# Recording the program and issuing it in a list scheduler's order, in place of a weave with fitted step times

## The chip, the cores and the metric

One core of one Trainium2 chip runs one program. The metric is the device time of that program in microseconds; the kernel before was run three times, with a median of 1408.34 us (1407.92 to 1408.75). The engines named below are PE (TensorE: matmuls, with PEld for its weight loads), DVE (VectorE), ACT (ScalarE), POOL (GpSimd) and SP (which only issues DMAs). Each takes its own instructions strictly in the order in which the program gives them to it, and waits on semaphores for the others.

## The reference

One layer of a diffusion backbone on 1024 latent tokens of 1024 channels, with 256 context tokens:

```python
h_x = layer_norm(x) * (1 + scale_x) + shift_x              # adaLN from c; the same for ctx
p_x = split(h_x @ w_in)                                    # f_val, f_gate, qkv, dn_gate, beta, decay, r_f, r_d
y_f = fourier_branch(p_x[0], p_x[1])                       # 4 groups: Re(2-D DFT), linear map, SiLU gate, projection
y_d = deltanet_branch(qkv, dn_gate, beta, decay)           # 8 heads of 128, two directions
out = (sigmoid(r_f) * y_f + sigmoid(r_d) * y_d) @ w_out
x   = layer_norm(2**0.25 * x + gate_x * out) * ln_g + ln_b
```

The DeltaNet branch takes a short convolution and SiLU of q, k and v, and then, in chunks, solves a unit triangular system per chunk, direction and head, and scans the chunks with a 128x128 state:

```python
a_mat = strict_tril(kb @ k.T * decay) + I                  # per chunk
u, w  = triangular_solve(a_mat, [v * beta, kb * exp(gc)])
for chunk:                                                 # scan
    v_new = u - w @ S
    o     = (q * exp(gc)) @ S + qk @ v_new
    S     = S * exp(g_last) + k_dec.T @ v_new
```

The latent scans start from the final states of the context scans. All is in float32.

## The kernel before, in words

The program has three parts, one after the other, each with its own pool of on-chip buffers in the place of the last one's. **Head and Fourier branch**: `head` loads the tokens and adaLN's weights, normalises, transposes and modulates them into an operand of eight row blocks in two parts (`hh`, `hl`); then the context's k and v, the Fourier branch's blocks and its projections run. **DeltaNet heads** (pool `dn`): eight heads, one after the other. **Tail**: the DeltaNet output projection, the merge, the output projection and the last layer norm.

A product with weights is done in "blocks" of 128 output channels by 1024 tokens (`latent`, L192): 8 contraction steps by 2 halves by 3 passes (`mm3y`, L124: lines L127, L130 and L133), 48 matmuls of 512 columns into a `main` tile, of which PSUM holds two. Their weights come by `weight` (L178): a 512 KB load, a cast by ACT in two halves (L188), and a subtraction by POOL (L189); two sets of buffers.

A head's own work is a chain (`deltanet` L671, `inverse` L724, `scan` L818):

- `zp` (L688 on PE, L692 on DVE) from k, q and the decay factors E, which `decays` (L703) loads from DRAM (L708), masks on POOL (L710) and exponentiates on ACT (L714). E has four buffers for a head's five pairs of chunks.
- `inverse`: a stream transpose into X (L736), 30 steps of DVE (L748, L751), a transpose back (L755), two rounds of small matmuls 32 to 64 (L774, L784, with transposes L789 and L790 behind them), and two rounds 64 to 128 (L802, L810) with copies by ACT between them.
- `scan`: ten steps. Each is PE (L840), DVE (R, L842), PE (L854), ACT (L856), PE (L869), DVE (S, L873), in two directions side by side, with L850, L861, L863 and L881 beside it.

`zp`, `kdec`, `acc`, `ktok` and the state tiles have one buffer, so the next head's `zp` starts when this scan is done. While the chain of head h runs, the program also does the projections of head h+1 (k, q, v, and the output gate of head h) with their convolutions, norms and transposes (`qkv_jobs`, L596), and one, two or five of the sixteen merge blocks (`TAKE`): mostly six blocks a head. The end of head h-1 (`finish`, L893) is done within head h's X steps.

What sets the order around the change: Python writes instructions in program order, and that is the order on each engine. The chain is a generator that yields where PE may take other work; the blocks are a second generator that yields after every three matmuls. `weave` (L248) runs the chain to its next yield, looks up that yield's entry in a table of fitted times (`STEPS`, 89 entries; `STEPS_LAST` for head 7; `TABLES` for the gate tables; `FIN` for the end), times a fitted factor per head (`RATES`), and issues block matmuls worth that many microseconds. Whatever a block brings with it on DVE, ACT, POOL and SP is written at the place where its last matmul falls.

```python
        for _ in lead:
            owed += next(times) * rate
            while owed > 0:
                q = next(fill, None)
                ...
                owed -= q
```

Of the kernel before, what the change touches and what calls it, by code (L numbers as in the profile page):

```python
# [27 lines left out]
TABLES = (9.2, 8.15, 1.41, 5.3)  # L28
STEPS_LAST = (0.354, 0.604, 2.165, 0.754, 0.454, 1.602, 0.427, 0.511, 1.07, 1.452, 0.19, 0.0, 0.694, 1.883, 0.935, 0.771, 1.001, 1.231, 0.803, 1.117, 1.529, 1.062, 0.606, 1.002, 0.821, 0.0, 0.776, 0.623, 0.595, 0.854, 0.526, 0.486, 0.182, 0.492, 2.076, 0.247, 1.65, 0.0, 0.0, 0.0, 0.0, 1.894, 0.04, 0.0, 0.0, 0.0, 2.162, 0.0, 0.38, 0.0, 1.134, 0.15, 0.821, 0.0, 0.0, 0.377, 0.12, 0.0, 1.081, 0.378, 0.0, 0.54, 0.77, 0.0, 0.54, 0.378, 0.242, 0.6, 0, 0.269, 0.45, 0.57, 0.269, 0.0, 0.378, 0.569, 1.0, 0.12, 0.269, 0.4, 0.378, 0.242, 0.648, 0.574, 0.722, 0.0, 1.0, 0.269, 2.7)
STEPS = (0.204, 0.604, 0.604, 0.604, 0.604, 1.187, 0.427, 0.511, 1.07, 0.662, 0.19, 1.19, 0.844, 2.033, 0.785, 0.921, 0.851, 1.231, 0.803, 1.267, 1.979, 0.0, 1.056, 1.614, 0.821, 0.8, 0.776, 0.623, 0.595, 0.854, 0.826, 0.486, 0.332, 0.042, 1.276, 0.397, 1.65, 0.0, 0.0, 0.0, 0, 1.426, 0.04, 0.0, 0.468, 0.0, 2.162, 0.8, 0.0, 0.0, 1.134, 0.0, 0.021, 0.0, 0.0, 0.135, 0.27, 0.0, 0.931, 0.378, 0.392, 0.54, 0.378, 0.242, 0.84, 0.078, 0.242, 0.6, 0.0, 0, 0.45, 0.57, 0.538, 0.0, 0.378, 0.569, 0.55, 0.77, 0.269, 0.6, 0.378, 0.242, 0.39, 1.378, 1.202, 0.12, 0.0, 1.1, 3.119)  # L30
FIN = 0.292
RATES = (0.966, 1.34, 1.34, 1.34, 1.34, 1.23, 1.666, 1.33)
# [30 lines left out]

class Net:
    def __init__(self, tc, es, a, out, dbg=None):
        self.tc, self.es, self.a, self.out = tc, es, a, out
        self.nc = tc.nc
        self.dbg = dbg or {}

    def pool(self, name, bufs=1, es=None, **kw):  # L70
        return (es or self.es).enter_context(self.tc.tile_pool(name=name, bufs=bufs, **kw))

    def dump(self, name, ap, idx=None):
        if name in self.dbg:
            dst = self.dbg[name]
            if idx is not None:
                dst = dst[idx]
            if ap.dtype == F32R:
                ap = ap.bitcast(F32)
            self.nc.sync.dma_start(out=dst, in_=ap)  # L80

# [1 line left out]
    def rsqrt(self, pool, x, shape, tag):  # L83
        """1 / sqrt(x) of a small float32 tile: Newton steps from an integer seed."""
# [32 lines left out]
    def mm3(self, ps, lh, ll, rh, rl, first, last):  # L117
        """ps += (lh + ll)^T (rh + rl) in three float32r passes."""
# [5 lines left out]
    def mm3y(self, ps, lh, ll, rh, rl, first, last):  # L124
        """The same, giving TensorE away in between."""
# [11 lines left out]
    def constants(self):  # L137
# [21 lines left out]
        # adds up four blocks of 32 rows  # L159
# [32 lines left out]
    def latent(self, src, rhs, k, done):  # L192
        """A block of weights times the latent tokens' operand: quanta of PE work, then done(PSUM)."""
# [24 lines left out]
    def plain(self, f):  # L218
        """Work that needs no weights, as a job."""
        def job(w):  # L220
            f()
            yield 0.0
        return None, 0, job

    def after(self, f):
        """The same for work in several parts."""
        return None, 0, lambda w: f()

    def stream(self, jobs, first=None):
        """Run jobs in order, the weights of the next one under way; first: the first one's, if they are."""  # L230
# [17 lines left out]
    def weave(self, lead, fill, rate, times):  # L248
        """fill takes TensorE between the lead's steps: after each, rate times its entry of times."""
        owed = 0.0  # L250
        times = iter(times)
        for _ in lead:
            owed += next(times) * rate
            while owed > 0:
                q = next(fill, None)
                if q is None:
                    owed = float("-inf")
                    break
                owed -= q

# [1 line left out]
    def pe_add(self, x, rows, ec, eng=None):  # L262
        """x += the tokens' position code: the grid's rows in one half of the channels, its columns in the other."""
# [1120 lines left out]
```

## Time and profile before

| what | value |
|---|---|
| time, median of 3 runs | 1408.34 us |
| span of the profiled execution | 1409.0 us, no time of its own beside it |
| PE busy | 1296.9 us (92%) |
| PE weight loads busy | 1050.7 us (75%) |
| DVE busy | 967.8 us (69%) |
| ACT, POOL busy | 555.9, 451.1 us |
| granted PE clock, mean of the span | 0.959 |
| DMA | 129.91 MB, 92 GB/s |

How to read it: a matmul's record runs from its start to a modelled end, and consecutive matmuls overlap, so that PE's busy share counts time in which a matmul is still draining and no next one has started. What PE needs is read from the distance between starts in a dense stretch. The chain of waits follows back from the last instruction to what released each one.

### The profile page before, as it was taken

Reading aid. Unit: us, or ns where it says so; the run is one execution under the profiler, and the core shown is the slowest. Engines: PE = TensorE matmul, PEld = TensorE weight load, DVE = VectorE, ACT = ScalarE, POOL = GpSimd, SP = SyncE. Lnnn points to the kernel's source line nnn. Section 1 sums busy time; section 2 is a strip of 40 time slices with the busy share of each in tenths; the row PEclk is TensorE's granted clock in tenths of the full one; section 3 lists DMA queues with packets and bytes.
Section 4 is the critical chain, followed back from the end, with each engine's and each line's share of the span. In section 5 each row is a group of like instructions: output and inputs, shape, how many; then the busy total and the mean of one; then the engine's idle time right before and its main releaser. Section 6 shows DMA issues by size and latency. Waiting matters only on the chain.

```text
span 1409.0 us, 22686 instructions
## 1 busy us (share of the span) xinstructions
PE 1296.9 (92%) x8274; PEld 1050.7 (75%) x8274; DVE 967.8 (69%) x2664; ACT 555.9 (39%) x1499; POOL 451.1 (32%) x358
## 2 busy tenths in 40 slices
PE   7899999999789989889899998988998999999997
PEld 1487787887678768768777876876876877888786
DVE  6776554308876965984894795697697494744997
ACT  2643333335444444443544444345354343521200
POOL 3532332135523222430440332223243122234610
PEclk9999999999899999989998999999998999999999
DMA  8434332342211211311311211121120032375431
GB/s 316 152 97 119 115 111 91 125 169 78 65 39 44 69 46 48 88 61 38 83 58 56 53 62 66 50 79 54 35 79 31 31 113 75 120 264 162 160 124 60
DMA packets 51892, 129.91 MB, mean 92 GB/s; under 512 B 6242, under 2 KB 18915, under 8 KB 51780
## 3 DMA queue, kind: packets, MB, share of 16 engines
q1 hardware_dynamic: 44496, 114.02, 26.1%
q10 hardware_dynamic: 7284, 14.45, 3.0%
q8 instruction: 65, 1.06, 0.3%
q14 instruction: 47, 0.39, 0.1%
HBM read 105.29 MB, written 23.15 MB: 91 GB/s over the span
## 4 chain that ended last, share of the span: by engine, by line
PE 50%; DVE 33%; DMA 6%; ACT 5%; POOL 3%; issue 3%; ACTq 0%; SPq 0%; DVEq 0%; POOLq 0%
PE main L127 8%; PE main L133 8%; PE main L130 8%; DVE X L751 7%; DVE B L748 6%; DMA E<-gr 3%; PE s L854 3%; PE s L869 3%; PE s L840 2%; PE s L881 2%; PE s L850 2%; DVE cv L553 2%; POOL E L710 2%; DVE cv L552 2%; PE main L120 2%
## 5 line engine op out<-in xcount | busy, mean ns | idle before, releaser
L127 PE MATMUL main<-h,whi 128*128 128x512 f32 x1008 | 424.8, 421 | 6.2 <-DVE cv L553 6.2
L133 PE MATMUL main<-h,wlo 128*128 128x512 f32 x1008 | 410.8, 408 | 0.1
L130 PE MATMUL main<-l,whi 128*128 128x512 f32 x1008 | 410.2, 407 | 0.0
L127 PEld LDWEIGHTS main<-h,whi 128*128 128x128 f32 x1008 | 196.2, 195 | 42.9 <-ACT th L554 5.8
L189 POOL TENSOR_TENSOR wlo<-wraw,whi 128x1024 fp32r<-128x1024 f32 x48 | 127.7, 2660 | 307.1 <-ACT whi L188 295.0
L133 PEld LDWEIGHTS main<-h,wlo 128*128 128x128 f32 x1008 | 195.5, 194 | 40.5 <-POOL wlo L101 0.5
L130 PEld LDWEIGHTS main<-l,whi 128*128 128x128 f32 x1008 | 196.0, 194 | 32.8
L751 DVE TENSOR_TENSOR X<-X,B 128x110 f32<-128x110 f32 (+27 forms) x472 | 120.6, 292 | 0.0
L748 DVE TENSOR_TENSOR B<-X 128x110 f32<-128x110 f32 (+27 forms) x472 | 111.8, 274 | 0.0
L101 POOL TENSOR_TENSOR wlo<-wraw,whi 128x512 fp32r<-128x512 f32 (+1 forms) x40 | 49.8, 1245 | 180.9 <-ACT whi L100 172.2
L710 POOL TENSOR_TENSOR E<-E,mask 128x256 f32<-128x256 f32 x80 | 67.2, 866 | 89.7 <-DMA E<-gr 62.0
L188 ACT CAST whi<-wraw 128x512 fp32r<-128x512 f32 x96 | 59.4, 623 | 79.7 <-PE main L130 71.4
L100 ACT CAST whi<-wraw 128x512 fp32r<-128x512 f32 (+1 forms) x80 | 44.7, 575 | 109.1 <-PE main L130 73.5
L554 ACT ACTIVATE th<-cv 128x512 f32<-128x512 f32 (+1 forms) x64 | 36.9, 576 | 124.6 <-DVE cv L553 124.4
L714 ACT ACTIVATE E<-E,nG 128x128 f32<-128x128 f32 x160 | 52.7, 392 | 68.2 <-POOL E L710 67.7
L692 DVE SCALAR_TENSOR_TENSOR zp<-s,c,E 128x256 f32<-128x256 f32 (+1 forms) x160 | 64.5, 452 | 21.6 <-ACT E L714 14.6
L101 DVE TENSOR_TENSOR wlo<-wraw,whi 128x512 fp32r<-128x512 f32 (+1 forms) x40 | 36.9, 923 | 61.4 <-ACT whi L100 48.2
L699 POOL TENSOR_TENSOR kdec<-ktok,ce 128x1280 f32<-128x1280 f32 x16 | 37.0, 2326 | 130.6 <-PE s L869 128.3
L873 DVE SCALAR_TENSOR_TENSOR S<-S,egl,s 128x128 f32<-128x128 f32 x128 | 40.0, 344 | 54.9 <-PE s L869 53.2
L856 ACT COPY zp<-s 128x128 f32<-128x128 f32 x144 | 36.3, 273 | 80.3 <-PE s L854 80.3
L552 DVE SCALAR_TENSOR_TENSOR cv<-main,cst,cv 128x511 f32<-128x511 f32 (+1 forms) x48 | 35.3, 735 | 39.6 <-ACT cv L549 39.6
L842 DVE SCALAR_TENSOR_TENSOR R<-s,eG,vt 128x128 f32<-128x128 f32 x144 | 45.3, 347 | 22.5 <-PE s L840 19.1
(343 smaller groups left out, 2560.3 us busy)
## 6 DMA issues: line engine op xcount, KB each, us to landing
wraw<-in_win SPq DMA_DIRECT2D x72, 512.0 KB, 3.5
E<-gr SPq DMA_DIRECT2D x40, 256.0 KB, 4.7
wmod<-in_wm SPq DMA_DIRECT2D x32, 256.0 KB, 5.4
x<-in_x SPq DMA_DIRECT2D x8, 512.0 KB, 5.4
wgate<-in_wg SPq DMA_DIRECT2D x8, 512.0 KB, 3.9
yf<-yf ACTq DMA_DIRECT2D x8, 512.0 KB, 2.8
rfy<-yf SPq DMA_DIRECT2D x8, 512.0 KB, 4.5
af<-rfy SPq DMA_DIRECT2D x8, 512.0 KB, 2.6
```

Source lines behind the costliest of these rows:

```text
L101: (eng or self.nc.gpsimd).tensor_tensor(out=lo, in0=x, in1=hi.bitcast(F32), op=ALU.subtract)
L127: mm(ps, lhsT=lh, rhs=rh, start=first, stop=False)
L130: mm(ps, lhsT=lh, rhs=rl, start=False, stop=False)
L133: mm(ps, lhsT=ll, rhs=rh, start=False, stop=last)
L188: self.nc.scalar.copy(out=hi[:, i:i + n], in_=raw[:, i:i + n])
L189: self.nc.gpsimd.tensor_tensor(out=lo[:, :k], in0=raw[:, :k], in1=hi[:, :k].bitcast(F32), op=ALU.subtract)
L552: v.scalar_tensor_tensor(out=x[:, a:hi], in0=ps[:, a - 1:hi - 1], scalar=w(0), in1=x[:, a:hi], op0=ALU.mult, op1=ALU.add)
L692: v.scalar_tensor_tensor(out=o, in0=ps.rearrange("p (a i) -> p a i", a=W), scalar=G.c[:, d, u:u + 1], in1=e[:, d, i].unsqueeze(1).to_broad ...
L710: nc.gpsimd.tensor_tensor(out=e[:, d], in0=e[:, d], in1=self.mask[:, d].unsqueeze(1).to_broadcast([P, 2, P]), op=ALU.add)
L714: nc.scalar.activation(out=e[:, d, i], in_=e[:, d, i], func=AF.Exp, bias=self.nG[:, 8 * d + h, u:u + 1])
L748: v.tensor_tensor(out=B, in0=X[:, c0::2, l:l + 1].to_broadcast([P, w, l]), in1=X[:, l:l + 1, :l].to_broadcast([P, w, l]), op=ALU.mult)
L751: v.tensor_tensor(out=X[:, c0::2, :l], in0=X[:, c0::2, :l], in1=B, op=ALU.subtract)
```

## The change

The class `Net`, which writes the kernel, is nearly as it was. In place of the real engines and pools it is given a `Recorder`, whose engines note each call as an `Op` with its engine, buffers and cost, and whose tiles (`View`) note which elements of a buffer are read and written. From that come the dependencies. `schedule` then simulates the engines: at each step it takes the engine that can start an instruction earliest, and on it, of the instructions that are ready, the one with the longest chain of cost behind it (`rank`). `issue` makes the real calls in order of their planned starts. `weave`, its tables and `RATES` are gone; generators are simply run to their end (`drain`), blocks first, then the chain, then the finish. The context's transposed tiles get buffers of their own (tag `cT` in place of `x`), the `junk` tile is left out of the dependencies (`loose`), and each PSUM tile of four `s` banks and two `main` ones gets a fixed bank by the plan. All operations, their sizes and their engines stay, as do `TAKE`, the job lists and `ORDER`, in which buffers of one tag are handed out.

```diff
-TABLES = (9.2, 8.15, 1.41, 5.3)
-STEPS_LAST = (0.354, 0.604, 2.165, ...)
-STEPS = (0.204, 0.604, 0.604, ...)
-FIN = 0.292
-RATES = (0.966, 1.34, 1.34, 1.34, 1.34, 1.23, 1.666, 1.33)
+HOP, SAME = 60, 35
+BANKS = dict(main=2, s=4)
...
+    def touch(self, o, v, write):
+        ...
+        for q, w, a0, a1, m in b.log:
+            over = a0 < p1 and p0 < a1 and m & bits
+            if over and (write or w) and q is not o:
+                same = q.eng == o.eng and not q.bytes and (b.psum and o.eng == "PE" or not w)
+                o.pred[q] = max(o.pred.get(q, 0), 1 if same else 2)
...
+    def finish(self):
+        ...
+                    if i:
+                        first.order.add(held[i - 1].ops[0]) if tag != "s" else None
+                    ...
+                    n = b.kw["bufs"] or p.bufs
+                    if i >= n:
+                        for q in held[i - n].ops:
+                            first.pred[q] = max(first.pred.get(q, 0), 2)
+            if p.before:
+                gone = {q for x in p.before for q in x.ops}
+                ...
+                for o in heads:
+                    for q in gone:
+                        ...
+    def ranks(self):
+        for o in reversed(order):
+            o.rank = o.lat
+            for s in o.succ:
+                k = s.pred[o]
+                d = o.occ if k == 1 else o.lat + (SAME if s.eng == o.eng else HOP)
+                o.rank = max(o.rank, d + s.rank)
+            for s in o.follow:
+                o.rank = max(o.rank, s.rank)
...
+    def schedule(self):
+        ...
+        while len(done) < len(self.ops):
+            best = None
+            for e in ENGINES:
+                ...
+                if pick and (best is None or pick[0] < best[0]):
+                    best = (pick[0], e, pick[1])
+            ...
+            o.start = t
+            free[e] = t + o.occ
+            o.end = t + o.lat
+            if o.bytes:
+                dma = max(dma, t + 400) + o.bytes / o.rate
+                o.end = max(t + 2000, dma + 1600)
+            if o.lock:
+                locked["POOL" if e == "DVE" else "DVE"] = o.end
+            ...
+        done.sort(key=lambda o: o.start)
+        return done
...
+    def issue(self, order):
+        ...
+        with tc.manual_schedule():
+            for i, o in enumerate(order):
+                ...
+                call = getattr(engine[o.eng], o.method)
+                at(o.line)(call, [real(v) for v in o.args], {k: real(v) for k, v in o.kw.items()})
...
+def cost(eng, method, args, kw, out, ins):
+    if method == "dma_start":
+        ...
+        return (110 if eng == "SP" else 90), 2000, False, n, (120 if many else 300)
+    if eng == "PE":
+        if method == "transpose":
+            occ = 112
+        else:
+            if r.dtype == F32R:
+                occ = 11.5 + 0.421 * cols
+            elif r.dtype == F32:
+                occ = 4 * (2 + cols / 2.4) * (0.5 if k == 64 and m == 64 else 0.3 if k == 32 and m == 32 else 1)
+        return occ, occ + 175, False, 0, 0
+    if eng == "DVE":
+        lat = 155 + n / (1.92 if one else 0.96) + 50 * psum
+        return lat - 75, lat, one or two, 0, 0
+    if eng == "ACT":
+        lat = 180 + n / 1.2 + (110 if any(size(v) == 1 for v in ins) and n > 16 else 0) + (160 if "accum_out" in kw else 0)
+        return lat - 95, lat, False, 0, 0
+    lat = 110 + n * (2.25 if two else 1.08) if method != "memset" else 100 + n
+    return lat, lat + 20, method != "memset", 0, 0
...
-    def weave(self, lead, fill, rate, times):
...
+    @staticmethod
+    def drain(*parts):
+        for part in parts:
+            for _ in part:
+                pass
...
-                    two = [sp.tile([P, 4, NX], F32, tag="x", name="cT", bufs=8) for _ in range(2)]
+                    two = [sp.tile([P, 4, NX], F32, tag="cT", name="cT", bufs=2) for _ in range(2)]
...
-                fill = self.stream(jobs)
+                self.drain(self.stream(jobs), self.deltanet(h, Gs[h], iter(())))
                 if h + 1 == HEADS:
-                    fill = itertools.chain(fill, self.heads_out())
-                self.weave(self.deltanet(h, Gs[h], side), fill, RATES[h], STEPS if h + 1 < HEADS else STEPS_LAST)
-                for _ in side:
-                    pass
-                side = self.finish(h, Gs[h])
-                ...
+                    self.drain(self.heads_out())
+                self.drain(self.finish(h, Gs[h]))
...
-def body(tc, a, out, dbg=None):
+def body(tc, a, out):
+    rec = Recorder(tc)
     with ExitStack() as es:
-        Net(tc, es, a, out, dbg).run()
+        Net(rec, es, a, out).run()
+    rec.issue(rec.schedule())
```

## Rows read from the trace of the kernel before

**Rows 1.** The page: busy time of each engine; shares of the chain that ended last.
```profile
PE 1296.9 (92%) x8274; PEld 1050.7 (75%) x8274; DVE 967.8 (69%) x2664; ACT 555.9 (39%) x1499; POOL 451.1 (32%) x358
...
PE 50%; DVE 33%; DMA 6%; ACT 5%; POOL 3%; issue 3%; ACTq 0%; SPq 0%; DVEq 0%; POOLq 0%
```
**Rows 2.** Stages: window, its length, each engine's busy us (instructions), clock, DMA share, GB/s.
```profile
0.00:82.00 82.00, 66.67 (x276) 31.94 (x277) 62.40 (x122) 39.98 (x68) 39.34 (x33) 0.94 0.57 201
82.00:322.00 240.00, 229.58 (x1228) 193.85 (x1226) 108.86 (x205) 86.07 (x181) 67.28 (x88) 0.99 0.39 122
322.00:343.00 21.00, 20.04 (x103) 16.25 (x102) 16.24 (x34) 11.49 (x37) 14.90 (x8) 1.00 0.14 48
343.00:445.00 102.00, 90.28 (x689) 74.80 (x688) 77.69 (x249) 43.81 (x131) 39.07 (x25) 0.93 0.22 58
...
676.00:791.50 115.50, 106.00 (x760) 87.22 (x760) 84.02 (x264) 50.66 (x153) 34.68 (x27) 0.94 0.20 60
...
1126.00:1228.50 102.50, 96.37 (x718) 79.54 (x717) 71.69 (x236) 44.26 (x124) 29.22 (x20) 0.98 0.32 102
1228.50:1409.00 180.50, 169.63 (x772) 140.54 (x771) 126.16 (x239) 27.91 (x47) 58.95 (x32) 0.99 0.46 153
...
1200.00:1300.00 100.00, 99.54 (x509) 84.02 (x509) 52.07 (x93) 31.82 (x75) 35.43 (x20) 1.00 0.58 192
```
**Rows 3.** The chain that ended last, whole run: start us, us, what (heads 0, 3, 6, 7).
```profile
396.31 1.94 DVE C L755
...
409.49 1.15 PE s L810 x32
...
675.98 1.30 PE s L688 x6
...
691.30 2.11 DVE X L736
...
722.82 2.10 DVE C L755
...
751.52 1.18 PE s L810 x32
...
790.62 1.06 PE s L881 x8
...
1094.23 1.08 PE s L810 x32
1125.32 1.03 PE s L881 x8
1127.28 1.26 DVE zp L692 x3
...
1140.22 2.07 DVE X L736
...
1168.18 1.92 DVE C L755
```
**Rows 4.** Groups by line and shape on PE in head 3 (676 to 791.5 us).
```profile
L127 PE MATMUL main<-h,whi 128*128 128x512 f32 x96 | 42.0, 437 | 0.0
...
L854 PE MATMUL s<-R,zp 128*128 128x128 f32 x36 | 5.7, 281 | 0.0
```
**Rows 5.** Timeline of dense block matmuls, 27 starts apart: start us, us, instruction.
```profile
300.05 0.39 PE L130 MATMUL main<-l,whi 128*128 128x512 f32 x1
...
306.17 0.39 PE L130 MATMUL main<-l,whi 128*128 128x512 f32 x1
```
**Rows 6.** The chain within head 3 alone, one piece of PE's scan work.
```profile
778.49 0.89 PE s L881 x8
```
**Rows 7.** Timeline of head 3 between its small matmul rounds, two DVE instructions.
```profile
734.84 2.31 DVE L88 TENSOR_SCALAR dnrt<-se 128x10 int32<-128x10 int32 x1
...
742.02 0.51 DVE L789 STREAM_TRANSPOSE T<-s 32x320 f32<-32x320 f32 x1
```
**Rows 8.** All instructions on the low weight parts: durations in ns, min/median/max.
```profile
L189 POOL TENSOR_TENSOR wlo<-wraw,whi x48: 2340/2394/5321, 296.4 to 1175.1; 128x1024 fp32r<-128x1024 f32 x48
```

More of the change, by code (lines that the diff above doesn't have):

```diff
@@ L1 @@
+import heapq
 import itertools
+import sys
 from contextlib import ExitStack
@@ new lines, with __init__ @@
+BANKS = dict(main=2, s=4)
+class Buf:
+    __slots__ = ("pool", "kw", "shape", "dtype", "n", "tag", "ops", "log", "real", "slot", "psum", "free", "loose", "gang")
+    def __init__(self, pool, shape, dtype, tag, loose=False, **kw):
+        self.pool, self.shape, self.dtype, self.tag, self.kw, self.loose = pool, list(shape), dtype, tag, kw, loose
+        self.ops, self.log, self.real, self.slot, self.psum = [], [], None, None, pool.space == PSUM
+        self.free, self.gang = int(np.prod(shape[1:])), tag == "s"
@@ new lines, with __init__, tile @@
+class Pool:
+    def __init__(self, rec, name, bufs, space, before):
+        self.rec, self.name, self.bufs, self.space, self.before = rec, name, bufs, space, before
+        self.tags, self.ops, self.real, self.guard, self.kids, self.left = {}, [], None, None, [], 0
+        self.up = None
+    def tile(self, shape, dtype, tag=None, name=None, bufs=None, loose=False):
+        tag = tag or name
+        b = Buf(self, shape, dtype, tag, loose, name=name, bufs=bufs)
+        held = self.tags.setdefault(tag, [])
+        b.n = len(held)
+        held.append(b)
+        if self.space == DRAM:
+            return View(b, None, (0, shape[0]), (), dtype)
+        return View(b, np.arange(b.free).reshape(shape[1:]), (0, shape[0]), (), dtype)
@@ new lines, with at @@
+ENGINES = ("PE", "DVE", "ACT", "POOL", "SP")
+_at = {}
+def at(line):
+    if line not in _at:
+        space = {}
+        exec(compile("\n" * (line - 1) + "def issue(f, a, k): f(*a, **k)", __file__, "exec"), space)
+        _at[line] = space["issue"]
+    return _at[line]
+def cost(eng, method, args, kw, out, ins):
+    size = lambda v: int(np.prod(v.idx.shape))
+    if method == "dma_start":
+        v = next(v for v in out + ins if v.idx is not None)
+        n = size(v) * (v.p[1] - v.p[0]) * 4
+        many = any(s[0] == "partition_broadcast" for w in ins for s in w.chain)
+        return (110 if eng == "SP" else 90), 2000, False, n, (120 if many else 300)
+    n = max([size(v) for v in out + ins if v.idx is not None])
+    if eng == "PE":
+        cols = size(out[0])
+        if method == "transpose":
+            occ = 112
+        else:
+            l, r = (kw[k] for k in ("lhsT", "rhs"))
+            if r.dtype == F32R:
+                occ = 11.5 + 0.421 * cols
+            elif r.dtype == F32:
+                k, m = r.p[1] - r.p[0], int(np.prod(l.idx.shape))
+                occ = 4 * (2 + cols / 2.4) * (0.5 if k == 64 and m == 64 else 0.3 if k == 32 and m == 32 else 1)
+            else:
+                occ = 3 + cols / 2.4
+        return occ, occ + 175, False, 0, 0
+    psum = any(v.buf.psum for v in out + ins)
+    two = sum(1 for v in ins if not v.buf.psum and size(v) > 1) > 1
+    if eng == "DVE":
+        one = method in ("tensor_copy", "tensor_scalar", "memset") and not psum
+        lat = 155 + n / (1.92 if one else 0.96) + 50 * psum
+        if method == "transpose":
+            lat = 150 + n * 1.9 if n > 900 else 180 + n
+        return lat - 75, lat, one or two, 0, 0
[4 more added lines that the diff above has]
+    return lat, lat + 20, method != "memset", 0, 0
@@ L83, in rsqrt, with __init__, pool @@
+FIRST = sys._getframe().f_lineno
+class Net:
+    def __init__(self, rec, es, a, out):
+        self.nc, self.es, self.a, self.out = rec, es, a, out
+    def pool(self, name, bufs=1, es=None, space=None):
+        p = self.nc.pool(name, bufs, space)
+        (es or self.es).callback(self.nc.close, p)
+        return p
     def rsqrt(self, pool, x, shape, tag):
@@ L592, in norms @@
         for i, u in enumerate(units):
-            junk = self.dn.tile([P, P], F32, tag="junk", name="junk")
+            junk = self.dn.tile([P, P], F32, tag="junk", name="junk", loose=True)
             self.nc.scalar.activation(out=junk, in_=ps[:, i * P:(i + 1) * P], func=AF.Square, accum_out=ss[:, u:u + 1])
@@ L1256, in run @@
                 fill = self.stream(four + outs)
-                self.weave(self.tables(bd, sp), fill, 1.0, TABLES)
-                for _ in fill:
-                    pass
+                self.drain(self.tables(bd, sp), fill)
             self.both = False
```

350 lines of the change are left out of this document (310 added, 40 removed).

## The prediction

> **What bounds the kernel now.** I read the page first. PE is busy for 92% of the span and the chain that ended last lies on PE for 50% and on DVE for 33% [rows 1]. So neither "PE is full" nor "a DVE chain" is the whole answer, and the stages have to be separated. The windows by stage [rows 2] show that a head is 115.5 us long in the middle (head 3, 676 to 791.5), with PE busy 106.0 and DVE 84.0, and that the tail, from 1228.5 on, is filled on PE to within 11 us.
>
> Busy is not need, since records of matmuls overlap. In a dense stretch 27 block matmuls start within 306.17 - 300.05 = 6.12 us, 0.227 each [rows 5], while each record is 0.39 long. Head 3 has 96 records on each of three such lines, 288 x 0.227 = 65.4 us [rows 4]. Scan and set-up products of 128 columns take 0.89 / 8 = 0.111 a record [rows 6]; there are 176 of them on five lines like L854's [rows 4], 19.5 us. The other small ones (16 of 256 columns at twice 0.111, 28 transposes at 0.111, 80 of 64 columns at 0.036 to 0.06, 160 of 32 columns) come to about 12. PE needs 97 us of these 115.5. Six blocks of weights are in it; one more or less is 48 x 0.227 = 10.9, so a head with five needs 86. Counted in this way over all records, PE needs 741 us in the eight heads (343 to 1228.5, 885.5 us), 19 in the 21 before them, 216 of 240 in the Fourier stage, 59 of 82 at the start and about 171 of 180.5 in the tail: 1206 us of 1409. The heads hold 144 of the 203 that are not needed.
>
> Why they are not used is in the chain [rows 3]. Head 3: 675.98 to 691.30 for zp (15.3), to 722.82 for the X steps (31.5), to 751.52 for the small rounds up to L810 (28.7), to 791.68 for the scan (40.2): 115.7 in all, so the chain is the period. But other heads do the same stages faster: zp 12.9 and X steps 28.0 in head 7 (1127.28, 1140.22, 1168.18), the small rounds 13.2 in head 0 (396.31 to 409.49), the scan 32.1 in head 6 (1094.23 to 1126.35). The sum of the fastest is 86.2. The 29 us between are waits behind other work on the same engine: in head 3 the transpose L789 starts at 742.02, behind a small DVE instruction of the next head's norms that took 2.31 us at 734.84 and a convolution's after it [rows 7], and the whole round takes twice what head 0's takes.
>
> **The change, part by part.** No operation is added or taken away on any engine, so the 1206 us of PE work stay; only order can pay.
>
> *Heads.* The order of the fill was set by quanta of three matmuls, 0.68 us, put in by a table that seven heads share, and a block's convolution on DVE came where its last matmul fell. Now each engine takes the ready instruction with the longest chain behind it. The head chain has eight stages of 86 us or more ahead of it, the fill of the next head only its own few; the chain goes first everywhere and waits at most for the one instruction that is running (0.23 on PE, up to 1.2 on DVE). The chain then fits into less than PE's 97, and PE becomes what ends a head. How full can PE be? The floor of the stage 322 to 1228.5 is 19 + 741 = 760 us, 84% of its 906.5. The Fourier stage, with little chain in it, runs at 216 / 240 = 0.90, the tail at 171 / 180.5 = 0.95 [rows 2]; I take 0.93, between the two nearest. 760 / 0.93 = 818, a gain of 88.5 us, with 0 (0.84, as now) and 122 (0.97) as the ends. A middle head would be about 104.5 us.
>
> *Fourier stage, 82 to 322.* The same 0.93: 216 / 0.93 = 232, a gain of 8 (0 to 17). Its job order is kept, and heads' buffers still lie in the place of this stage's, so head 0 can't start early; a wait for four pools' last instruction stays.
>
> *Start, 0 to 82.* It waits for 16 MB of weights and tokens (82 us at 201 GB/s, a DMA share of 0.57 [rows 2]). `ORDER` no longer orders the loads, their ranks do. The loads in a wrong order cost a wait such as stands here now; I take 0, from +10 (two late groups) to -10 (not quite half of the 23 us that PE doesn't need). The context's own buffers take away a wait for token slots within this; nothing by itself.
>
> *Tail.* PE is dense at 99.54 of 100 us in 1200 to 1300 [rows 2]; what remains is the last layer norm behind the last matmul. I take 0 (-7 to +7).
>
> *Queues and waits.* Some 330 DMA issues move, on SP past each other: E's loads, the stores of og, td and af, and the weights are one queue, now ordered by planned starts; a weight load that waits for its buffer still holds what is behind it. DVE and POOL get exclusive prices for two-input work. The bank of each PSUM tile is fixed by the plan. Their bounds are in the 0.84 to 0.97 above; each alone I can't price better than nothing to some 10 us either way.
>
> Sum: 1409.0 - 88.5 - 8 = 1312.5 on the profiled execution, whose span is 0.7 above the median of the runs: **1312 us**.
>
> A rule weighed against this: PE's page row says 92%, its weight loads 75% [rows 1]. The Trainium skill ("Perfetto Trace Analysis", Identifying the Most-Contended Engine) holds matmul busy time for a bad measure of headroom and the share of weight loading for a good one. Read alone it would put the floor at 1050.7 us, well below the sum above. No stretch here bears that out: in the densest 100 us, with matmuls back to back, weight loads stand at 84.02 [rows 2], so the rule's floor is rather 1050.7 / 0.84 = 1251, and I give 1051 no chance.
>
> **The rivals.**
>
> *Near the floor.* Ranks are global and PE is filled to 0.97 throughout: 760 / 0.97 = 783 (-123), Fourier 223 (-17), start -8: 1261. For it: the tail does it now, and the granted clock in the heads, 0.93 to 0.98 [rows 2], would rise with fewer gaps. Against: two `main` tiles and two sets of weights still bound how far fill can run ahead.
>
> *DVE takes PE's place.* DVE is busy 84 of 115.5 us in head 3 [rows 2]. About 41 of that are zp and the X steps, which are DVE's nearly throughout, and I put 20 more into scan and small rounds; the 23 left (an estimate: convolutions, norms, the gate) are outside the chain; if they can't hide beside the PE and ACT stages of it, a head lasts 86.2 + 23 = 109, and the stage gains 8 x 6.3 = 50; with half of that given back by the lead-in and the E loads, the time is about 1375. For it: an instruction on DVE can't be broken off, and one of 10 columns took 2.31 us there [rows 7]. Against: rounds and scan, 13 + 32 us, leave DVE those 20 short of full, 25 us for 23.
>
> *Slower: late operands in a tight order.* The weave leaves block matmuls between chain steps, so a late operand costs nothing on PE. A plan that puts the chain's matmul where its operand is just due makes PE, and the fill queued behind it, wait for each lateness. Place: the hand-overs to PE in a head, 60 in the scan (10 steps, 3 products, 2 directions) and about 10 elsewhere, 560 in all. It decides from 96 / 560 = 0.17 us mean lateness. At 0.25 us it costs 140: 1409 - 96 + 140 = 1453. For it: the plan knows neither the half clock (0.93 in head 0, 0.94 in head 3 [rows 2]) nor a subtraction of 5321 ns where its price is 110 + 2.25 x 1024 = 2414 [rows 8]. Against: that price is the row's median, 2394, the price of a block matmul, 11.5 + 0.421 x 512 = 227 ns, is the row's 0.227 [rows 5], and lateness on one chain partly cancels.
>
> *It doesn't do what it says.* Buffers of a tag are still handed out in recorded order, which might hold everything where it is: 1409, within 0.2%, about what can be told from no change in this kernel.
>
> **How the numbers follow.** My forecast, a PE filled to 0.90 to 0.96 in the heads (1280 to 1345), 0.48; near the floor (1235 to 1280), 0.16; DVE (1345 to 1405), 0.18; no change 0.03; slower, mostly to 1420 to 1480, 0.15. So faster by over 0.2% is 0.82, same 0.03, slower 0.15. The range of 8 in 10 leaves out the lower third of the floor case and the slower case: 1250 to 1405.
>
> **What would show it.** X transposes (L736) of the middle heads 100 to 108 us apart in place of 115.6; the small rounds, from L755 to the first scan product, near 20 us in place of 33; PE's busy share at 95% or more in the heads' windows, with the same counts of matmuls; the granted clock nearer to 1; the tail as long as before. I am wrong if heads stay above 111 us apart (DVE, or late operands: told apart by whether PE's idle time is ended by DVE's R, S and zp or by convolutions being ahead of them), or if the start or the tail grows by more than 10 us.

## The result, and the profile after

The changed kernel takes **1488.21 us** (1487.78 to 1492.36, 4 runs) against 1408.13 us of the kernel before beside it: a ratio of **1.0587**, 95% interval 1.0565 to 1.0609. It is 5.9% slower, where 1312 us was forecast. The profiled execution has a span of 1486.0 us, 77.0 more than before.

The page, first the span, then PE's busy time and the clock in 40 slices:

```profile
span 1486.0 us, 22655 instructions
...
PE 1293.6 (87%) x8274; PEld 1047.5 (70%) x8274; DVE 931.1 (63%) x2664; ACT 561.9 (38%) x1499; POOL 491.5 (33%) x358
...
PEclk9989999999799799899899899899899699999998
```

Read PE's row beside [rows 1]: the same 8274 instructions, and 3.3 us less busy time. What grew is the time in which PE is not busy, from 1409.0 - 1296.9 = 112.1 us to 192.4. That is 80 us, the whole loss. So the question is what PE waits for.

The stages, each head from its first `zp` product to the next one's (columns as in [rows 2]):

```profile
310.00:358.70 48.70, 48.16 (x217) 39.77 (x218) 21.47 (x32) 23.11 (x60) 24.45 (x19) 1.00 0.42 132
358.70:463.10 104.40, 86.43 (x679) 72.03 (x678) 78.08 (x255) 42.41 (x123) 40.28 (x26) 0.90 0.16 46
463.10:561.60 98.50, 79.52 (x660) 67.07 (x659) 73.35 (x256) 45.10 (x143) 37.23 (x25) 0.90 0.16 49
561.60:670.70 109.10, 97.89 (x735) 80.89 (x735) 78.36 (x266) 52.98 (x162) 36.07 (x25) 0.95 0.22 64
670.70:787.10 116.40, 103.75 (x754) 85.85 (x753) 79.10 (x263) 52.09 (x156) 41.70 (x26) 0.94 0.22 60
787.10:904.00 116.90, 103.43 (x761) 86.09 (x760) 77.76 (x266) 51.54 (x154) 42.73 (x26) 0.94 0.21 59
...
1130.20:1279.70 149.50, 124.53 (x833) 102.29 (x832) 70.02 (x243) 50.92 (x138) 25.41 (x18) 0.90 0.21 66
1279.70:1486.00 206.30, 178.71 (x791) 145.56 (x789) 136.00 (x243) 31.64 (x53) 66.36 (x36) 0.95 0.42 144
```

The first head starts at 358.7 in place of 343.0 [rows 2] (+15.7). Heads 0 to 6 together take 771.5 us in place of 783.2 (-11.7); the full ones, 3 and 4 here, last 116.4 and 116.9, no shorter than 115.5. The 11.7 us are no gain: heads 1 and 2 are shorter because they leave work out, with 660 and 735 matmuls where the same heads issued 757 and 762 before. Head 7 takes 149.5 in place of 102.3 (+47.2), the tail 206.3 in place of 180.5 (+25.8). Head 7 and the tail issue 1624 matmuls where they issued 1490: some of their loss is this left-over block work (134 x 0.227 us [rows 5], about 30 us), the rest is PE standing still (25 and 28 us of it, 6 and 11 before).

Groups by line on PE: the first of a block's three products per step, then three products of the scan (after the first `|` busy us and mean ns, after the second the idle time just before them and what ended it):

```profile
L602 PE MATMUL main<-h,whi 128*128 128x512 f32 x1008 | 407.1, 418 | 90.8 <-DVE silu L1035 39.4 <-DVE B L1215 21.3 <-ACT th L1021 14.0
...
L1321 PE MATMUL s<-R,zp 128*128 128x128 f32 x288 | 57.2, 280 | 0.6 <-DVE R L1309 0.2
L1336 PE MATMUL s<-zp,kdec 128*128 128x128 f32 x288 | 55.6, 279 | 1.1 <-ACT zp L1323 0.9
L1307 PE MATMUL s<-S,kq 128*128 128x128 f32 x256 | 50.3, 278 | 0.8 <-DVE S L1340 0.7
```

The chain's products hardly wait: 2.5 us on these three lines. The block's do: 90.8 us, where the same line had 6.2 in the kernel before:

```profile
L127 PE MATMUL main<-h,whi 128*128 128x512 f32 x1008 | 424.8, 421 | 6.2 <-DVE cv L553 6.2
```

What ends that wait is an instruction of DVE or ACT that reads a `main` tile (`silu`, a convolution, the `th` behind one) or the X steps (`B`) ahead of it: both `main` tiles are full, and nobody empties them.

One such wait, the timeline of head 4, five of its lines (start us, us, instruction; in brackets the idle time before it):

```profile
813.05 13.98 POOL L664 TENSOR_TENSOR wlo<-wraw,whi 128x1024 fp32r<-128x1024 f32 x2 [5.28 <-ACT whi L663]
...
820.66 1.01 ACT L1034 ACTIVATE silu<-main 128x1024 f32<-128x1024 f32 x1
...
822.44 4.70 DVE L1218 TENSOR_TENSOR X<-X,B 128x99 f32<-128x99 f32 x2
...
830.19 1.21 DVE L1035 SCALAR_TENSOR_TENSOR silu<-silu,main 128x1024 f32<-128x1024 f32 x1
...
831.46 0.79 PE L602 MATMUL main<-h,whi 128*128 128x512 f32 x1 [10.97 <-DVE silu L1035]
```

ACT has done its part of the gate at 821.67. DVE's part, 1.21 us long, could follow at once, but the X steps have the longer chain and go first, until 830.19; PE, whose next block needs that bank, stands for 10.97 us. (One of these pairs of X steps took 4.70 us in place of some 0.4, held up by POOL's subtraction: theory B below.) The granted clock is then at its half level for a while:

```profile
822.30:836.00 13.70, 4.54 (x11) 3.58 (x12) 13.70 (x44) 2.63 (x5) 5.54 (x3) 0.50 0.29 77
```

Where does the work go that PE didn't do? Windows of the three parts of head 4's chain behind `zp` (X steps; small rounds, up to the first scan product; scan, up to the next `zp`), all instructions:

```profile
801.00:833.00 32.00, 19.97 (x94) 15.92 (x93) 31.47 (x132) 12.02 (x32) 19.21 (x7) 0.83 0.28 73
833.00:854.90 21.90, 20.84 (x297) 16.38 (x296) 8.67 (x20) 10.57 (x25) 2.60 (x4) 0.93 0.07 25
854.90:904.00 49.10, 48.71 (x310) 42.51 (x309) 27.20 (x85) 22.98 (x80) 12.06 (x7) 1.00 0.18 60
```

and L602 alone in them, a third of the block's matmuls (PE's and its loads' columns only):

```profile
801.00:833.00 32.00, 10.71 (x27) 5.11 (x26) 0.83 0.28 73
833.00:854.90 21.90, 8.25 (x19) 3.66 (x18) 0.93 0.07 25
854.90:904.00 49.10, 15.88 (x37) 7.05 (x37) 1.00 0.18 60
```

The same windows of the kernel before, head 3, L127 alone (here too the small rounds end at the first scan product, 4.2 us behind the L810 at which the prediction's sum of stages ends them):

```profile
691.30:722.80 31.50, 15.19 (x37) 7.44 (x38) 0.95 0.22 74
722.80:755.70 32.90, 11.48 (x25) 5.02 (x25) 0.84 0.15 49
755.70:791.50 35.80, 9.38 (x20) 3.83 (x20) 1.00 0.12 38
```

and its X steps with all instructions:

```profile
691.30:722.80 31.50, 29.16 (x131) 23.73 (x131) 31.48 (x137) 13.92 (x37) 8.34 (x5) 0.95 0.22 74
```

The X steps are no shorter (32.0 for 31.5), and during them PE is busy for 19.97 us in place of 29.16. Ten steps of the block fewer fall into them and six fewer into the small rounds, and 17 more into the scan: 17 x 3 x 0.227 us [rows 5] = 11.6 us, and the scan with what follows is 13.3 us longer, with PE full at 48.71 of 49.10. The small rounds did get shorter by 11.0 us, as forecast; the scan gives that back, and the head's period stays.

### The profile page after: what moved, and what is told of

The parts are those of the page before. It is cut to its first block, busy times and chain, and to the rows that moved or that the text cites. A ratio compares the mean times of both kernels' runs of the same rounds, so it can differ in the third digit from the quotient of the medians.

```text
span 1486.0 us, 22655 instructions
## 1 busy us (share of the span) xinstructions
PE 1293.6 (87%) x8274; PEld 1047.5 (70%) x8274; DVE 931.1 (63%) x2664; ACT 561.9 (38%) x1499; POOL 491.5 (33%) x358
## 5 line engine op out<-in xcount | busy, mean ns | idle before, releaser
L602 PE MATMUL main<-h,whi 128*128 128x512 f32 x1008 | 407.1, 418 | 90.8 <-DVE silu L1035 39.4
L605 PE MATMUL main<-l,whi 128*128 128x512 f32 x1008 | 402.1, 413 | 0.0
L608 PE MATMUL main<-h,wlo 128*128 128x512 f32 x1008 | 400.2, 413 | 0.0
L664 POOL TENSOR_TENSOR wlo<-wraw,whi 128x1024 fp32r<-128x1024 f32 x48 | 173.7, 3623 | 385.8 <-ACT whi L663 174.1
L602 PEld LDWEIGHTS main<-h,whi 128*128 128x128 f32 x1008 | 194.4, 194 | 130.9 <-DVE silu L1035 41.4
L1218 DVE TENSOR_TENSOR X<-X,B 128x110 f32<-128x110 f32 (+27 forms) x472 | 125.4, 305 | 0.0
L1215 DVE TENSOR_TENSOR B<-X 128x110 f32<-128x110 f32 (+27 forms) x472 | 99.7, 250 | 0.0
L576 DVE TENSOR_TENSOR wlo<-wraw,whi 128x512 fp32r<-128x512 f32 (+1 forms) x40 | 40.4, 1023 | 68.2 <-ACT whi L575 67.3
L1309 DVE SCALAR_TENSOR_TENSOR R<-s,eG,vt 128x128 f32<-128x128 f32 x144 | 50.1, 348 | 41.6 <-PE s L1307 40.0
L1177 POOL TENSOR_TENSOR E<-E,mask 128x256 f32<-128x256 f32 x80 | 58.9, 765 | 38.8 <-DMA E<-gr 25.7
L1321 PE MATMUL s<-R,zp 128*128 128x128 f32 x288 | 57.2, 280 | 0.6 <-DVE R L1309 0.2
```

The source lines that it names most:

```text
L602: mm(ps, lhsT=lh, rhs=rh, start=first, stop=False)
L605: mm(ps, lhsT=lh, rhs=rl, start=False, stop=False)
L608: mm(ps, lhsT=ll, rhs=rh, start=False, stop=last)
L664: self.nc.gpsimd.tensor_tensor(out=lo[:, :k], in0=raw[:, :k], in1=hi[:, :k].bitcast(F32), op=ALU.subtract)
L1177: nc.gpsimd.tensor_tensor(out=e[:, d], in0=e[:, d], in1=self.mask[:, d].unsqueeze(1).to_broadcast([P, 2, P]), op=ALU.add)
L1215: v.tensor_tensor(out=B, in0=X[:, c0::2, l:l + 1].to_broadcast([P, w, l]), in1=X[:, l:l + 1, :l].to_broadcast([P, w, l]), op=ALU.mult)
```

## The experiments

Three theories. **A**: the order is at fault. The rank is the longest chain of dependencies, and a PSUM tile's bank is not among them, so that the emptying of a `main` tile ranks below the X steps. In `finish` (the comment is added here):

```python
                    if b.psum:
                        first.opens = (first.opens or []) + [b]
                        continue                    # no edge from a bank's users to its next user
```

**B**: POOL and DVE hold each other up: a weight's subtraction lasts up to 11.7 us beside X steps.

```profile
L664 POOL TENSOR_TENSOR wlo<-wraw,whi x48: 2351/2389/11667, 309.4 to 1236.7; 128x1024 fp32r<-128x1024 f32 x48
```

**C**: something else in the machinery (fixed banks, issue order) costs, whatever the priority.

**e1, the emptying first.** All else stays.

```diff
+        for o in self.ops:
+            if o.eng != "PE" and any(b.tag == "main" for b in o.bufs):
+                o.rank += 1e6
```

> The changed kernel with one line more: after the ranks are made, every instruction of DVE, ACT or POOL that reads or writes a main tile gets a rank above all others, so that the emptying of a main tile no longer waits behind the X steps. Theory A (the rank knows nothing of the PSUM bank that an instruction frees, so PE stands still for about 11 us in each head and the fill that it could have done falls into the scan): PE's idle time before the first matmul of a block falls from 90.8 us to under 40, the scans of heads 3 to 5 from 46 us to under 40, and the time from 1488 to 1400 to 1440. Theory B (the order is tight, and its operands come late because DVE and POOL hold each other up): PE's gaps change places, the time stays within 15 us of 1488.

1436.83 us, 1.0199 (1.0167 to 1.023) of the kernel before: 51 us off. The row that had 90.8:

```profile
L605 PE MATMUL main<-h,whi 128*128 128x512 f32 x1008 | 404.3, 416 | 29.9 <-DVE silu L1038 9.7 <-DVE t L1597 8.6 <-DVE cv L1023 6.1
```

61 us of waiting gone, 51 of them from the time. A is two thirds of the loss; the kernel is still slower than before.

**e2 and e3, the weave put back.** Both record the program with `weave` and its tables, as the kernel before writes it. e2 issues in recorded order; e3 keeps the list scheduler, with the place in the recording as priority.

```diff
 # e3; the weave and its tables, put back, are left out here
-        self.ranks()
+        self.sorted_ops()
+        for o in self.ops:
+            o.rank = -o.n
```

> The recorder and its issue of a fixed order, with the step tables and the weave put back, and the recorded order issued as it stands (the earliest recorded instruction whose predecessors are issued and for which a bank is free); no list scheduler. If the machinery (fixed banks, buffers of the context, a fixed order) costs nothing, this is the kernel before again: 1400 to 1420. If the machinery is the loss (a third theory, C): over 1450.

> The list scheduler as it is, with its prices and its bank model, but its priority is the place in the weave's recorded order (weave and tables put back for the recording) in place of the longest chain behind an instruction. Theory A, the priority is what is wrong with the change and list scheduling as such is not: under 1420. Theory B, any order as tight as this one is loses by late operands: 1460 or more, with X steps (L1218's successor line) at 300 ns a piece as in the changed kernel.

e2: 1796.85 us, 1.275 (1.271 to 1.279), a miss. The order of the calls, issued as it is, is not the kernel before: its engines get their instructions in another order than its Python writes them, against what stands above under the kernel before. In the traces of the two, compared by operation and tile names, only 992 of DVE's 2664 instructions and 268 of ACT's 1499 stand at the same place of their engine's order. What makes that order was not tried. e3: **1376.4 us, 0.977 (0.9742 to 0.9798)**, faster than before. So C is out: recording, fixed banks and the scheduler are all in e3. What differs from the changed kernel is the priority, and with the weave the order in which buffers of a tag are handed out; the two are worth 112 us.

**e4 and e6, the subtractions off POOL.** The 48 low weight parts are set to zero by a memset; the low parts are thereby left out of the product's result, not its matmuls. e4 has the changed kernel's plan, e6 the plan of e1.

```diff
-            nc.gpsimd.tensor_tensor(out=lo, in0=raw, in1=hi, op=ALU.subtract)
+            nc.gpsimd.memset(lo.bitcast(F32), 0.0)
```

> The changed kernel in its own planned order on every engine, with the 48 subtractions on POOL that make the low parts of the heads' weights (3623 ns each there) left out: a memset of the same tile stands in their place, which reads nothing. The outputs are then wrong in the low part of these weights. Theory B: the X steps' second instruction falls from 305 to about 245 ns, and the time by 40 us or more. Theory A: PE waits for the same emptied banks, and the time falls by less than 20.

> Emptying of main tiles first (1436.8) together with the heads' 48 POOL subtractions left out (1454.0 alone; the low parts of these weights are zero). If the two losses are separate, 1488 - 51 - 34 = 1403, within 12. If the hold-ups between POOL and DVE only cost where a main tile waits to be emptied, more than 1420.

e4: 1453.99 us (1.0324, 1.0291 to 1.0358), 34 less, between the 20 of A and the 40 of B. The second instruction of the X steps, in the changed kernel and in e4:

```profile
L1218 DVE TENSOR_TENSOR X<-X,B 128x110 f32<-128x110 f32 (+27 forms) x472 | 125.4, 305 | 0.0
```

```profile
L1223 DVE TENSOR_TENSOR X<-X,B 128x110 f32<-128x110 f32 (+27 forms) x472 | 95.1, 242 | 0.0
```

It fell from 305 to 242 ns, as B had it. e6: 1412.33 (1.0033, 1.0012 to 1.0055), 24 less than e1, so that the two losses nearly add up. B is a real cost, but the smaller, and taking it away doesn't bring the kernel below the one before.

**e7 and e8, B in the good order.** e3 with the subtraction on DVE, and with half on each.

```diff
-            self.nc.gpsimd.tensor_tensor(out=lo[:, :k], ...)
+            for i, e in ((0, self.nc.gpsimd), (n, self.nc.vector)):   # e8; e7: all on vector
+                e.tensor_tensor(out=lo[:, i:i + n], ...)
```

> List scheduling with the weave's recorded place as priority (1376.4), the heads' weight subtractions moved from POOL to DVE in two halves each. Theory B: POOL's two-input work holds up DVE's X steps and the reverse (its subtraction took up to 9.9 us there against 2.4 alone); without it the X steps' second instruction falls from 278 to about 245 ns, and 1376 becomes 1345 to 1370 although DVE gets 48 x 1.3 = 62 us more. If the contention costs less than the added DVE work: 1380 to 1400.

> The same with half of each subtraction on POOL and half on DVE. Theory B: shorter holds on both, 1355 to 1375. Against it: unchanged, 1370 to 1385, since POOL's half waits for DVE's X steps as the whole did.

1390.39 us (0.9876, 0.984 to 0.9913) and 1387.15 (0.9846, 0.9805 to 0.9887), both above e3: POOL is the better place for them, held up or not.

**e5, e10, e11: where longest chain does harm.** e5 is e1 with recorded places as priority ahead of the first head and behind the last; e10 is the changed kernel with that at the start alone; e11 records with the weave and takes the longest chain, emptying first, in heads 0 to 5 only.

```diff
 # e11 (e5: no weave, s == 1 in all heads, the boost everywhere)
+            s = 0 if o.n < a else 1 if o.n < b else 2
+            o.rank = (o.rank / 100 if s == 1 else -o.n) + 1e6 * (2 - s)
+            if s == 1 and o.eng != "PE" and any(b.tag == "main" for b in o.bufs):
+                o.rank += 1e7
```

> The changed kernel (its own recording, no weave) with the emptying of main tiles first, as in the run of 1436.8 us, and beside that the recorded place as priority for everything recorded before the first head and after the last one; the heads keep the longest chain. Theory A says that the longest chain is a poor priority at both ends too (first zp at 359 in place of 343, tail of 206 us in place of 180): 1400 to 1418. If the ends are long for another reason (the last head's late scan alone): 1430 or more.

> The changed kernel, with the recorded place as priority only for what is recorded ahead of the first head; everything else keeps its longest-chain rank. If the start is a cost of its own (the first head starts at 358.7 us in place of 343.0), the first head starts near 342 us, as it did in the two runs whose start went by recorded place (342.3 and 340.0), and the time is 1470 us, plus or minus 8. If the late start only moves block work that must be done anyway, the heads get longer by what the start gains and the time stays within 6 us of 1488.

> The weave's recorded order is kept, and the list scheduler's priority is the recorded place at the start, in the last two heads and in the tail; in heads 0 to 5 it is the longest chain with the emptying of `main` tiles first. If the longest chain is as good as the recorded place in the middle heads once banks are emptied in time, and only the ends need the recorded place, the time is 1365 to 1380 us, level with the 1376 us of the run whose priority is the recorded place throughout. If the longest chain costs something in the middle heads too (it draws block work ahead, so that the last heads lack it), the time is 1385 to 1410 us.

e5: 1392.17 us (0.9874, 0.983 to 0.9917), 45 below e1. e10: 1472.84 us (1.0458, 1.0431 to 1.0485); its first head starts at 339.5 and it is 15 us faster than the changed kernel, so the late start was lost time and not work done early. e11: **1370.03 us (0.9733, 0.97 to 0.9766)**, the fastest here, though its interval overlaps e3's: with banks emptied in time, longest chain is as good as the fitted weave in the middle heads, and no better to speak of.

**e9, the missing edge.** No boost; the rank gets an edge from a `main` tile's users to the opening of the tile two later.

```diff
+            for s in self.frees.get(o, ()):        # ops of a main tile -> first op of the tile after the next
+                o.rank = max(o.rank, o.lat + HOP + s.rank)
```

> The longest-chain rank gets one kind of edge that it lacked: from every instruction that uses a `main` tile of the block to the opening of the tile that takes the same bank two tiles later. No instruction is boosted by hand. If the missing edge is the cause (theory A, narrow form), the emptying of a bank gets its rank from the block's next products, the idle time before the block's first matmul falls from 90.8 us to about 30, as it did when the emptying was put first by hand (1437 us), and the time is 1437 to 1460 us. If longest chain is a poor order for the block whatever edges it has (theory A, wide form), the emptying still ranks below the X steps, that idle time stays above 60 us and the time stays above 1470 us.

```profile
L612 PE MATMUL main<-h,whi 128*128 128x512 f32 x1008 | 406.1, 417 | 76.8 <-DVE silu L1045 38.8 <-ACT th L1031 14.9 <-DVE B L1225 9.5
```

1462.18 us (1.0401, 1.0356 to 1.0446), between the two bands, half of what e1 gave. `silu` still ends 38.8 us of waiting, as in the changed kernel (39.4): with the edge its rank is that of the next block, and by that row this is still below the X steps'; the ranks themselves were not printed. The missing edge is part of the cause, not the whole: with it there for the `main` tiles, "the longest chain first" still lets PE stand.

**e13, the emptying late in the good order.** e3, with DVE's readers of `main` tiles ranked 600 recorded places later.

```diff
+            if o.eng == "DVE" and any(b.tag == "main" for b in o.bufs):
+                o.rank -= 600
```

> The 1376 us kernel (priority is the recorded place) with one thing put back: VectorE's instructions that read a `main` tile are ranked as if recorded 600 places later, about a quarter of a head, so that the X steps go ahead of them. If the late emptying of the two banks is what costs (theory A), it must cost in this good order too: the idle time before the block's first product rises from 23 us to 60 or more and the time to 1420 to 1470 us. If a poor longest-chain rank for everything else was the real cause and the emptying only went with it, the time stays within 15 us of 1376.

```profile
L611 PE MATMUL main<-h,whi 128*128 128x512 f32 x1008 | 418.4, 415 | 56.6 <-DVE cv L1042 30.7 <-DVE X L1240 11.6 <-DVE t L1616 8.3
```

In e3 the same row:

```profile
L609 PE MATMUL main<-h,whi 128*128 128x512 f32 x1008 | 414.9, 412 | 23.1 <-DVE t L1614 11.4 <-DVE cv L1040 6.0 <-ACT th L1041 2.7
```

1381.85 us (0.9826, 0.98 to 0.9852): the wait rose from 23.1 to 56.6 us, nearly as expected, the time by 5 only. A miss for A: PE's idle time as a whole rose from 98.8 to 108.1 us, so that 24 of the 33 us had been waits of PE elsewhere. A wait in that row is not by itself lost time. That left open whether "chain first" is the fault at all.

**e14, e15, e16: chain first, alone.** e3 with the head's chain (zp to scan) ranked 3000 places earlier: on every engine, on PE alone, and on every engine with the emptying ahead of it.

```diff
 # the line numbers of e16; in e14 and e15, two lines shorter, 1160 and 1381
+            if 1162 < o.line < 1383:                       # deltanet, decays, inverse, scan; e15: and o.eng == "PE"
+                o.rank += 3000
+            if o.eng != "PE" and any(b.tag == "main" for b in o.bufs):      # e16 only
+                o.rank += 6000
```

> The 1376 us kernel (priority is the recorded place) with the head's chain first on every engine: each instruction of zp, X steps, rounds and scan is ranked as if recorded 3000 places (more than a head) earlier, all else keeps its recorded place. Theory A (chain first is itself the fault, since the emptying of the two banks then waits until the X steps are over): main's idle time 70 us or more, heads 108 us or longer, 1410 to 1470 us. Theory D (the fault is how longest chain orders the rest: block work drawn ahead, ends left empty): the time stays within 15 us of 1376, as it did with the emptying 600 places late.

> The same, chain first on TensorE alone; VectorE, ScalarE and GpSimd keep the recorded place. Theory A: the fault lies on VectorE, so this costs little, 1366 to 1391 us, with main's idle time below 40 us. If chain first on TensorE is what pushes the block's products into the scan, the time is 1400 us or more.

> Chain first on every engine, and the emptying of `main` tiles ahead of the chain. Theory A: most of what chain first costs comes back, main's idle time below 40 us, 1370 to 1395 us. Theory D: no different from chain first alone, within 10 us of it.

e14: **1466.36 us** (1.0412, 1.0379 to 1.0444), 90 above e3. e15: 1377.66 (0.9788, 0.9762 to 0.9814), no different from e3. e16: 1400.04 (0.9938, 0.9918 to 0.9959), 66 of the 90 back, 5 us short of the range that A had for it. So A it is in the main: chain first costs, on PE alone it costs nothing, and most of what it costs elsewhere comes back when the emptying goes ahead of the chain. Late emptying without chain first had cost little (e13), so it is the two together. The first products of a block in e14, and in e16:

```profile
L611 PE MATMUL main<-h,whi 128*128 128x512 f32 x1008 | 417.4, 415 | 109.5 <-DVE silu L1057 75.7 <-DVE B L1237 18.4 <-ACT h L584 11.9
```

```profile
L613 PE MATMUL main<-h,whi 128*128 128x512 f32 x1008 | 415.0, 412 | 39.9 <-DVE cv L1044 13.7 <-ACT th L1045 13.1 <-ACT h L586 11.5
```

The mechanism is best seen in head 3, in windows of X steps, small rounds and scan with what follows to the next `zp`. e14, that block line alone:

```profile
680.40:711.00 30.60, 7.27 (x17) 3.26 (x17) 0.74 0.20 67
711.00:729.30 18.30, 6.61 (x16) 3.15 (x16) 0.97 0.01 2
729.30:784.10 54.80, 19.70 (x47) 8.90 (x47) 1.00 0.15 54
```

e3, the same:

```profile
668.50:716.10 47.60, 21.84 (x55) 10.50 (x54) 0.96 0.25 72
716.10:731.50 15.40, 4.94 (x12) 2.25 (x12) 1.00 0.09 36
731.50:762.60 31.10, 7.23 (x16) 3.06 (x16) 1.00 0.07 27
```

The good order has the *slower* X steps: 47.6 us for 30.6, since the block's emptying and the rest of the fill go in between. In return it has 31 steps of the block fewer left for the last window, which is 23.7 us shorter, and its head lasts 108.5 us against 119.8. The last window of e14, cut behind the scan's last product (764.6):

```profile
729.30:764.70 35.40, 8.91 (x21) 3.89 (x21) 1.00 0.18 68
764.70:784.10 19.40, 10.79 (x27) 5.01 (x27) 1.00 0.08 28
```

The scan itself is only 4.3 us longer there than e3's whole window. In the other 19.4 us the chain has ended, PE makes up 27 steps of the block, and the next head's `zp` starts only behind them, when the norms of its own k and q are there. Chain first speeds up the stage in which the chain needs nothing of PE, and leaves PE's work for a stretch in which PE is full (54.60 of the 54.80 us) and the chain, this head's or the next one's, waits for it.

e16 stays 24 us above e3. Its largest other waits on PE, 24.1 us, are for `acc` (the end of the head before) and `kq` (a convolution of the next head), which the chain also goes ahead of; this was not taken apart.

## Why the prediction was wrong

**The step that failed** is the heads': "the chain goes first everywhere and waits at most for the one instruction that is running (0.23 on PE, up to 1.2 on DVE). The chain then fits into less than PE's 97, and PE becomes what ends a head". It asked what the chain waits for, and not what waits for the chain. On DVE, which the X steps take for 32 us, it is the emptying of the two `main` tiles, with PE's next block behind it. So PE was not filled to 0.93 in the heads: from the first `zp` to the end of head 7 it took 921.0 us in place of 885.5, for about as many matmuls (5892 and 5902), and the prediction's need of 741 us over 921.0 is 0.80. The stage 322 to 1228.5 should have shrunk by 88.5 us; up to the end of head 7 the kernel got 51 us later. e14 shows the step by itself: chain first, added to e3's order, costs 90 us, where it was to gain 88.5.

The prediction had the limit in hand. Under the floor rival it wrote that "two `main` tiles and two sets of weights still bound how far fill can run ahead" and used it only against filling better than 0.93, not against filling worse than 0.84.

- *What it said would show it.* X transposes (L1203 now) 100 to 108 us apart: heads 3 to 5 are 116.4 to 118.0 long, wrong. Heads 1 and 2 came within it, by leaving block work over. Small rounds near 20 in place of 33 us: 21.9, right, and of no use. PE's share 95% in the heads: 88 to 89% in heads 3 and 4, wrong. Clock nearer to 1: 0.90 to 0.95, wrong, PE stands still for 11 us a head. Tail as long as before: +25.8, wrong. All its conditions for being wrong came true.
- *The start, 0 (-10 to +10), and the Fourier stage, a gain of 8.* Mis-sized: the last product on adaLN's weights (`s<-wmod,cs`) starts at 83.6 us in place of 67.6. From there to the first transposes of k and q it takes 257.5 us in place of 254.0, so the gain didn't come either. The first head is 15.7 us late with both together; e10 puts the price at 15.
- *The tail, 0 (-7 to +7).* Mis-sized: head 7 and tail lost 73 us. e5 won 45 against e1 with recorded places at both ends.
- *Late operands, the slower rival at 1453.* The side was right, the mechanism wrong: its 560 hand-overs wait 2.5 us in all on the three lines above, not 140.
- *DVE takes PE's place, 1375.* Wrong in its reason, since DVE's busy time fell to 931.1 us; right in that DVE decides, but by the order in it and not by its volume.
- *It doesn't do what it says, 1409.* Out: the order changed everywhere.
- *Its account of the kernel before.* It took the weave's table for the order on each engine; e2 shows that Python's order is not what ran.
- *Its sums.* 760 / 0.93 is 817 and 760 / 0.97 is 783, so the gains are 89 and 123 in place of 88.5 and 122. The zp of 12.9 us in head 7 is counted from the first DVE instruction; from the first product, as in head 3, it is 14.0, and the fastest stages come to 87.3. None of this moves the forecast by more than 1 us.
- *Right:* no work was added (the same 8274 matmuls), and a list scheduler can beat the weave: e3 and e11 do, by 2.3 and 2.7%, but take places from the weave's recorded order as priority; e5 does without it, by 1.3%. None comes near 1312: in e11 PE is still idle for 89.5 us.

The Trainium skill ("Perfetto Trace Analysis", Optimization Strategy) says of gaps that come back evenly on the engine that should be full that there may not be PSUM or SBUF for the next tile. The trace agrees: a wait of 10.5 to 11.0 us for a `main` tile or behind the X steps in each of heads 3 to 6. More tiles were not tried here; the same two, emptied in time (e1), left 29.9 us of 90.8.

## What to carry to other kernels

A list scheduler that ranks by the longest chain must count the buffers as dependencies, and even then the chain shouldn't go first on an engine that empties the fill's buffers: here an instruction of 1.2 us, kept waiting there, held up the bound engine for 11 us. Before pricing "the critical chain goes first", list on each engine what then goes second, and who stands behind that. And ask in which stage the bound engine's spare time lies: a stage that gets faster while the bound engine idles only moves its work to a stage that gets slower.

## What the runs showed of the hardware

- A subtraction of two SBUF operands on POOL, 2.39 us in the median, took up to 11.67 us beside DVE's dense X steps (5.32 before [rows 8]), and DVE is held in turn: a pair of X steps of 0.41 us took 4.70 in the timeline above and ended at 827.14, when POOL's two ended at 827.03. The Trainium skill ("SBUF — State Buffer", SBUF: two separate sides) has one port pair that one of the two holds for a whole instruction; the trace agrees in kind, and shows that the pricing of it in the plan, 2414 ns, can be nearly five times too low.
- A pause of PE costs beyond its end: PE stood from 820.5 to 831.46, and the granted clock was 0.50 from 822.3 to 836.0, so that the first blocks after the pause started 0.43 us apart (832.05, 832.48, 832.90) in place of 0.227 [rows 5].
